# A transformer kernel on one core: planner prices, two tables of plan parameters, and the place of one load

## The chip, the cores and the metric

The kernel runs on one core of one Trainium2 chip. The metric is the time of one execution on the device in microseconds (us). The kernel before took 3521.76, 3529.83 and 3524.83 us in three runs, a median of 3524.83 us.

## What is computed

Two transformer blocks over a sequence of 1024 tokens and a width of 1024, everything in float32. The first block has eight heads of latent attention, eight heads of dilated attention and sixteen experts. The second block has two layers, and each of them three kinds of attention over one projection. Cut to what matters here:

```python
def second_block(x, ctx, ...):
    for l in range(2):
        qa, ka, va, ga, qb, kb, vb, gb, qn, kn, vn, gn = split_proj(h @ w_in[l])
        # A: differential attention, 4 heads, 1024 + 256 context keys
        a = softmax(q0 k0) - lam * softmax(q1 k1);  oa = a @ va
        ya = rms_norm(oa, diff_subln[l]) * (1 - lam_init) * silu(ga)
        # B: grouped-query attention, 6 heads over 2 K/V heads
        yb = gqa_attend(qb, kb_all, vb_all) * silu(gb)
        # C: neighbourhood attention, 6 heads, windows of 8 x 16 in a grid, and the context
        yn = neighbourhood_attend(qn, kn, vn, kn_c, vn_c, nat_rpb[l], rows) * silu(gn)
        x = x + gt * (concat([ya, yb, yn]) @ w_out[l])
        # layer 0 also computes the three attentions for 256 context queries
```

## The kernel before

The program is a row of stages: the first block's projection, its attention, output projection, router and experts, and then for each layer of the second block a projection (`proj2`), the attention (`attn2`) and the output projection. The projections are long rows of matrix multiplications of split weights. They write their results into the arrays partA, partB, partC and the stacks of queries and keys in device memory, with stores (L1671, L1788) that the SyncE queue (SP) issues; the attention loads its tiles from there (L1936 for values and gates, L1943 for queries and keys, the latter on GpSimd's queue, POOL).

Inside an attention stage nobody writes the order of the instructions by hand. Each small group of instructions is an operation that is handed to a planner with `pl.op(prio, eng, fn, deps, bufs, dma)`: a priority, the engines that can do it with a price in microseconds for each, the function that issues it, the operations that it needs, its buffers, and the time of a transfer. `Plan.run` (L156) then goes through a simulated time: whenever an engine is free by the prices, it takes the ready operation with the lowest priority number whose buffers are free, and issues it. On every engine but SP the order so found is fixed. The prices and the priorities therefore set the order of the work, though not the time that it takes on the chip. Ahead of `run`, `Plan.early` (L144) issues a list of loads, which stand in front of everything in the plan.

The priorities come from the streams. In `attn2_open` (L1851) a layer has a stream "x", which holds three pairs of heads of the neighbourhood attention (`nat_tile`, L2301, 48 tiles) and then three of the grouped-query attention (`gqa_group`, L2232), and a stream "d" with the four heads of the differential attention (`stream_d`, `d_tile`). `TUNE` (L34) holds a row of parameters for each plan, "first" for the first block's attention and 0 and 1 for the layers: `lead` is how much earlier a load is wanted than its use, `aS`, `aD`, `aN` pull scores ahead, `pvx` and `pvd` push the multiplication by V back, `d0` and `df` set the start and speed of stream "d", `s`, `t` and `o` are how many banks of PSUM a kind of tile may hold.

Some names that the rest speaks of. xq, xk, xv and xP are the queries, keys, values and scores of stream "x", dq, dk, dv and dP those of "d"; s, w, t and o are tiles in PSUM: scores (s for "x", w for "d"), transposes (t) and outputs (o). L2323 makes a neighbourhood tile's scores, L2330 and L1933 on VectorE (DVE) their maxima, L2346 on ScalarE (ACT) the exponential; L317 is the transpose on TensorE (PE) and L2280 the multiplication by V. L2240, L2244 and L2245 make scores for the grouped-query heads (L2244 and L2245 as a pair into a t tile), L1030 is DVE's maximum over them, L1063 and L1067 what ACT and POOL or DVE do with the probabilities, L1998 their multiplication by V. L2092, L2096 and L2101 are the differential attention's scores, maxima and exponentials; L2032 and L2033 combine its two maps on POOL (L2030 is the same on DVE). At the end of each of its heads `d_finish` (L2145) computes a norm: a square on POOL (L2152), then on DVE a sum (L2156) and in `rstd_v` (L1837) thirteen operations (L1841 to L1848) on 128 x 10 numbers, as one operation of the plan with a price of 1.7 us, and then products on POOL (L2160).

The first value tile of stream "x", xv, is loaded by an operation in `pair` (inside `stream_x`, L2184), with a priority `lead` ahead of its use; the list that goes to `early` holds the keys, queries and tables (tb) of the first pair. Its buffers come out of pools by tag: xk, xq and tb from a pool (`ax1`) that is opened during the projection, all others from one that opens with the attention.

## Time and profile before

| | us |
|---|---|
| median of three runs | 3524.83 |
| lowest, highest run | 3521.76, 3529.83 |
| the profiled execution, its own time | 3530.24 |
| its span in the trace | 3528.2 |
| PE busy | 3339.7 (95%) |
| DVE busy | 2286.2 (65%) |
| ACT busy | 1711.5 (49%) |
| POOL busy | 1271.4 (36%) |
| mean granted clock of PE | 0.974 |

The profile shows one execution. Its span runs from the first to the last instruction, its own time also has what lies around them. Stages are told apart by their lines: the first block's attention lies between 255 and 865 us, layer 0's attention between 1905 and 2456, layer 1's between 2960 and 3424. In a list of waits, each row names the engine and the line that waited, the engine and result that ended the wait, the total, the number of times and the longest. In a timeline the columns are start, duration, engine, line, operation and tiles, and in brackets the idle time of the engine just ahead, with what ended it.

### The profile page before, as it was taken

The numbers are of one execution on the slowest core, as the hardware profiler recorded it, in microseconds if no ns is written. First come the engines' busy times: TensorE is split into PE (matmuls) and PEld (weight loads), VectorE is DVE, ScalarE is ACT, GpSimd is POOL, SyncE is SP. The second block draws the span as 40 slices with busy tenths as digits, with TensorE's granted clock in tenths as the row PEclk, the third lists the DMA queues.
The fourth block names the chain that finished last, engine by engine and source line by source line (L and its number), as shares of the span: only waits on it lengthen the run. The fifth ranks groups of instructions, "written<-read, shape, count | busy, mean of one in ns | idle before, by whom it ended". The sixth has DMA issues, their size and how long they took to land.

```text
span 3528.2 us, 50927 instructions
## 1 busy us (share of the span) xinstructions
PE 3339.7 (95%) x17832; PEld 2568.6 (73%) x17832; DVE 2286.2 (65%) x4884; ACT 1711.5 (49%) x3154; POOL 1271.4 (36%) x1103
## 2 busy tenths in 40 slices
PE   6998999988799999989999989999999999999999
PEld 5987666656588887779888665556899888765567
DVE  5524546544799998876770777876446821888762
ACT  4423545432388877753222666654333222776640
POOL 3211334332001010023451466756333521557761
PEclk9999999999899999999999999999999999999999
DMA  7338778575799999854353643114334354551133
GB/s 208 84 116 229 184 201 225 169 220 197 285 383 398 393 380 376 311 160 126 113 154 107 150 117 81 39 41 128 120 128 131 112 153 105 128 122 44 40 111 114
DMA packets 402451, 606.97 MB, mean 172 GB/s; under 512 B 77554, under 2 KB 283506, under 8 KB 398098
## 3 DMA queue, kind: packets, MB, share of 16 engines
q1 hardware_dynamic: 342772, 492.56, 41.9%
q0 software_dynamic: 26240, 94.13, 11.3%
q10 hardware_dynamic: 33184, 17.04, 1.7%
q8 instruction: 141, 2.31, 0.3%
q14 instruction: 114, 0.93, 0.1%
HBM read 479.10 MB, written 124.55 MB: 171 GB/s over the span
## 4 chain that ended last, share of the span: by engine, by line
PE 61%; DVE 7%; issue 2%; DMA 2%; POOL 2%; ACT 1%; SPq 0%; ACTq 0%; DVEq 0%; POOLq 0%
PE s L350 7%; PE t L317 6%; PE s L351 6%; PE s L349 6%; PE a L350 6%; PE a L351 6%; PE a L349 6%; PE o L1998 5%; PE o L2280 2%; PE w L2092 2%; PE s L2240 2%; PE s L2323 2%; PE t L2244 1%; PE t L2245 1%; PE t L2006 1%
## 5 line engine op out<-in xcount | busy, mean ns | idle before, releaser
L349 PE MATMUL a<-wh,h2H 128*128 128x384 f32 (+2 forms) x1280 | 460.5, 360 | 7.3 <-ACT wh L334 7.3
L1544 DVE TENSOR_TENSOR wl<-wr,wh 128x1024 fp32r<-128x1024 f32 x384 | 450.3, 1221 | 25.9 <-ACT wh L1543 19.3
L350 PE MATMUL a<-wl,h2H 128*128 128x384 f32 (+2 forms) x1280 | 453.7, 355 | 3.0 <-POOL wl L336 1.6
L351 PE MATMUL a<-wh,h2L 128*128 128x384 f32 (+2 forms) x1280 | 453.3, 354 | 1.7 <-POOL h2L L603 1.7
L1543 ACT ACTIVATE wh<-wr 128x1024 fp32r<-128x1024 f32 x384 | 394.7, 1058 | 75.2 <-PE s L351 73.7
L349 PEld LDWEIGHTS a<-wh,h2H 128*128 128x128 f32 x1280 | 243.1, 190 | 28.5 <-ACT wh L334 8.2
L350 PEld LDWEIGHTS a<-wl,h2H 128*128 128x128 f32 x1280 | 243.1, 190 | 24.9 <-POOL wl L336 2.5
L351 PEld LDWEIGHTS a<-wh,h2L 128*128 128x128 f32 x1280 | 242.6, 190 | 23.7 <-POOL h2L L603 2.1
L1067 POOL TENSOR_TENSOR xP<-xP,xPT 128x512 f32<-128x512 f32 x134 | 189.3, 1415 | 52.6 <-ACT xPT L1063 31.5
L350 PE MATMUL s<-wl,xH 128*128 128x512 f32 x512 | 202.0, 395 | 5.6 <-DVE wl L1544 5.2
L349 PE MATMUL s<-wh,xH 128*128 128x512 f32 x512 | 202.1, 395 | 0.0
L351 PE MATMUL s<-wh,xL 128*128 128x512 f32 x512 | 199.9, 390 | 0.0
L2096 DVE CUSTOM_DVE_ANT_0 dP<-w,zero 128x1280 f32<-128x1280 f32 x128 | 190.0, 1484 | 12.7 <-PE w L2092 9.9
L2101 ACT ACTIVATE dP<-dP,d 128x1280 f32<-128x1280 f32 x128 | 174.3, 1362 | 24.4 <-DVE d L2096 23.5
L1030 DVE TENSOR_REDUCE x<-s 128x1 f32<-128x512 f32 (+1 forms) x240 | 158.1, 684 | 31.9 <-PE s L2240 31.2
L1063 ACT ACTIVATE xPT<-t 128x512 f32<-128x512 f32 x240 | 132.1, 599 | 91.1 <-PE t L2245 78.5
L349 PE MATMUL s<-wh,yoH 128*128 128x512 f32 x416 | 167.6, 404 | 2.6 <-ACT wh L334 1.7
L336 POOL TENSOR_TENSOR wl<-wr,wh 128x1024 fp32r<-128x1024 f32 (+3 forms) x43 | 94.3, 2194 | 201.4 <-ACT wh L334 191.3
L350 PE MATMUL s<-wl,yoH 128*128 128x512 f32 x416 | 166.0, 399 | 0.8 <-DVE wl L336 0.8
L351 PE MATMUL s<-wh,yoL 128*128 128x512 f32 x416 | 165.1, 397 | 0.0
L1526 POOL DMA_INDIRECT xg<-h2d,idx x16 | 16.8, 1050 | 399.2 <-PE t L317 325.1
L336 DVE TENSOR_TENSOR wl<-wr,wh 128x1024 fp32r<-128x1024 f32 (+3 forms) x55 | 70.8, 1289 | 120.3 <-ACT wh L334 120.3
(463 smaller groups left out, 8363.8 us busy)
## 6 DMA issues: line engine op xcount, KB each, us to landing
wr<-in_w_gate_dram SPq DMA_DIRECT2D x128, 512.0 KB
wr<-in_w_up_dram SPq DMA_DIRECT2D x128, 512.0 KB
wr<-in_w_down_dram SPq DMA_DIRECT2D x128, 512.0 KB
aw<-in_w_ada_dram SPq DMA_DIRECT2D x32, 1024.0 KB
wr<-in_w_in_dram SPq DMA_DIRECT2D x50, 512.0 KB
aw<-in_w_ada_dram SPq DMA_DIRECT2D x32, 512.0 KB
wr<-in_w_in_dram SPq DMA_DIRECT2D x40, 384.0 KB
xk<-stackCk POOLq DMA_DIRECT2D x24, 640.0 KB, 10.6
```

What stands on the lines that cost most here:

```text
L317: self.nc.tensor.transpose(out, in_, self.ident[:n, :n])
L336: e.tensor_tensor(l, raw, h.bitcast(F32), ALU.subtract)
L349: nc.tensor.matmul(out, sH, h, start=first, stop=False)
L350: nc.tensor.matmul(out, sH, l, start=False, stop=False)
L351: nc.tensor.matmul(out, sL, h, start=False, stop=last)
L1030: nc.vector.tensor_reduce(dst, Sb.t[:, :n * w].rearrange("p (k c) -> p k c", k=n) if n > 1 else Sb.t[:, :w], AX.X, ALU.max)
L1067: eng.tensor_tensor(A.t[:, :512], PT.t[:, 0, :] if kb == 1 else A.t[:, :512], PT.t[:, kb, :], ALU.add)
L1543: nc.scalar.activation(h, raw, AF.Copy)
L1544: nc.vector.tensor_tensor(l, raw, h.bitcast(F32), ALU.subtract)
L1998: nc.tensor.matmul(O.t[a * 64:(a + 1) * 64, :], v(kb), PT[0](kb), start=(kb < 2), stop=(kb >= nb - 2))
L2096: nc.vector.tensor_tensor_reduce(Ps[i].t, W.t[:, :1280], self.zero.to_broadcast([P, 1280]), -1.0, 3e38, ALU.add, ALU.min, m["m"])
L2101: nc.scalar.activation(Ps[i].t, Ps[i].t, AF.Exp, bias=m["m"], scale=-1.0, accum_out=box[j][:, i:i + 1])
```

## The change

Three things change. The parameters of layers 0 and 1 in `TUNE` get new values. Prices of seven kinds of PE operation get new values; four of these (`st_group`, the transposes, the multiplications by V and the transposes back) are used in the first block's attention too, whose parameters stay as they are. And the first V tile moves into the pool that is open early, and its load into the list that is issued ahead of the plan. Cut to its core:

```diff
-    0: dict(lead=22.2, aS=54.6, aD=15.2, aN=47.2, st=0.4, pvx=21.6, pvd=16.7, d0=37.1, df=0.53, s=2, t=6, o=6),
-    1: dict(lead=13.3, aS=103.7, aD=14.6, aN=39.8, st=0.2, pvx=28.2, pvd=79.2, d0=14.4, df=0.5, s=2, t=4, o=2),
+    0: dict(lead=46.6315, aS=54.6, aD=17.6065, aN=54.9623, st=0.1169, pvx=20.343, pvd=0, d0=38.1898, df=0.53, s=2, t=9, o=4),
+    1: dict(lead=43.3625, aS=124.3762, aD=110.0272, aN=62.8556, st=0.1161, pvx=30.4682, pvd=59.8728, d0=10.0665, df=0.5317, s=2, t=4, o=7),
...
-            return pl.buf(tag, stream, lambda i: (pools.get(tag) or pools.get(tag[0]) or pools[rest]).tile(
+            return pl.buf(tag, stream, lambda i: (pools.get(f"{tag}{i}") or pools.get(tag) or pools.get(tag[0]) or pools[rest]).tile(
...
-                o = pl.op(p - self.q["aS"], {"pe": 0.02 + n * w * 0.0005}, mm, lds, [Sb] + QK)
+                o = pl.op(p - self.q["aS"], {"pe": 0.06 + n * w * 0.0005}, mm, lds, [Sb] + QK)
...
-        self.pools = {"xk": x1, "xq": x1, "tb": x1}
+        self.pools = {"xk": x1, "xq": x1, "tb": x1, "xv0": x1}
...
-            o = pl.op(p, {"pe": m * 0.107}, tr, [dep], [T, Pt, PT])
+            o = pl.op(p, {"pe": m * 0.115}, tr, [dep], [T, Pt, PT])
...
-            o = pl.op(p, {"pe": 0.89}, mm, list(deps) + [o], [O] + V)
+            o = pl.op(p, {"pe": 0.96}, mm, list(deps) + [o], [O] + V)
...
-        o = pl.op(p, {"pe": 1.7 if den else 0.8}, back, [o] + (den[0] if den else []), [oT, T] + (den[2] if den else []))
+        o = pl.op(p, {"pe": 1.0 if den else 0.84}, back, [o] + (den[0] if den else []), [oT, T] + (den[2] if den else []))
...
-            o = pl.op(p - self.q["aD"], {"pe": 0.71}, mm, lds, [W, Q, K])
+            o = pl.op(p - self.q["aD"], {"pe": 0.74}, mm, lds, [W, Q, K])
...
+                loads.append(vs[kind, p][1])
...
-        return loads[:5]
+        return loads[:6]
...
-        o = self.st_group("x", 2.95, 10, CH, s1, st, 0.43, [Q, K], [lq, lk, lm], Qm, lambda: Qm.t[64:68, i, :],
+        o = self.st_group("x", 2.95, 10, CH, s1, st, 0.5, [Q, K], [lq, lk, lm], Qm, lambda: Qm.t[64:68, i, :],
...
-        o = pl.op(p - self.q["aN"], {"pe": 0.88}, scores, [lq, K[0][1], K[1][1]], Sb + [Q, K[0][0], K[1][0]])
+        o = pl.op(p - self.q["aN"], {"pe": 1.9}, scores, [lq, K[0][1], K[1][1]], Sb + [Q, K[0][0], K[1][0]])
```

Lines from 2184 on stand one line further down in the changed kernel. The instructions are the same in both; what changes is where they stand. Two places are shown.

The first place is SP's queue where layer 0's attention begins (partA to partC are stores of the projection, vd its output tiles, dv, xv and xg loads of values and gates). Before:

```order
L1878 DMA subln_18174<-in_diff_subln_dram 128x64
L1671 DMA partC<-vd_18155 128x384
L1936 DMA dv_18191<-partA 128x10x64
L1936 DMA xv_18180<-partC 128x10x128
L1936 DMA xg_18185<-partC 128x4x128
L1936 DMA xgx_18187<-partC 128x2x128
```

And with the change, where the load of xv now stands, further up in the queue:

```order
L1788 DMA stackBk<-sL_17465 128x128
L1671 DMA partA<-vd_17503 128x256
L1936 DMA xv_17510<-partC 128x10x128
L2200 DMA tb_17518<-in_c_rpb_dram 128x1600
L2200 DMA tb_17520<-in_c_rpb_dram 128x1600
L1671 DMA partA<-vd_17556 128x256
```

The load of xv has moved from behind the projection's last store to a place ahead of both tables and of 21 stores.

The second place is PE where the fourth head of the differential attention ends in layer 0 (its DVE block, L2156 to L1848, is issued meanwhile). Before, the last result that DVE takes ahead of the block is the score tile s_22663, and PE's rows from there to these hold it, four pairs L2244 and L2245 and two short scores; these are the last twelve rows up to the first score tile (s_22745) that needs DVE after the block:

```order
L2245 MATMUL t_22685<-tb_22079,xk_20512 128x512
L2240 MATMUL s_22689<-xk_20805,xq_22481 128x512
L2244 MATMUL t_22691<-xq_22047,xk_20512 128x512
L2245 MATMUL t_22691<-tb_22079,xk_20512 128x512
L2244 MATMUL t_22713<-xq_22047,xk_20512 128x512
L2245 MATMUL t_22713<-tb_22079,xk_20512 128x512
L2244 MATMUL t_22718<-xq_22047,xk_20512 128x512
L2245 MATMUL t_22718<-tb_22079,xk_20512 128x512
L2398 MATMUL o_22722<-xPT_22465,xv_20018 64x256 x4
L317 MATMUL t_22733<-ident,sl_22605 4x128
L1998 MATMUL o_22735<-xPT_22574,xv_20018 64x512 x2
L2240 MATMUL s_22745<-xk_20805,xq_22481 128x512
```

With the change, from the last result that DVE takes ahead of the block (s_22723) to the first score tile that needs DVE after it (s_22789):

```order
L2241 MATMUL s_22723<-xk_20818,xq_22442 128x512
L317 MATMUL t_22727<-ident,oT_22593 128x128 x2
L317 MATMUL t_22735<-ident,sl_22601 4x128
L2241 MATMUL s_22737<-xk_20818,xq_22442 128x512
L1998 MATMUL o_22743<-xPT_22606,xv_20046 64x512 x2
L2241 MATMUL s_22747<-xk_20818,xq_22442 128x256 x2
L1998 MATMUL o_22743<-xPT_22606,xv_20046 64x512 x2
L2245 MATMUL t_22771<-xq_21990,xk_20818 128x512
L2246 MATMUL t_22771<-tb_22027,xk_20818 128x512
L1998 MATMUL o_22743<-xPT_22606,xv_20046 64x512 x4
L2241 MATMUL s_22789<-xk_20818,xq_22442 128x512
```

Seven pairs of score rows stood in this stretch before, and one stands there now, with eight steps of a multiplication by V.

## Rows read from the trace of the kernel before

**Rows 1.** Page, part 1: busy time, share of the span, instructions of each engine.

```profile
PE 3339.7 (95%) x17832; PEld 2568.6 (73%) x17832; DVE 2286.2 (65%) x4884; ACT 1711.5 (49%) x3154; POOL 1271.4 (36%) x1103
```

**Rows 2.** Windows: length, busy PE, PEld, DVE, ACT, POOL, granted clock, DMA share, GB/s.

```profile
255.00:865.00 610.00, 555.70 (x3185) 390.74 (x3184) 309.79 (x793) 258.54 (x658) 199.17 (x185) 0.95 0.71 204
1905.00:2456.00 551.00, 514.02 (x2855) 337.39 (x2853) 411.20 (x951) 322.17 (x647) 329.94 (x303) 0.96 0.35 88
...
2960.00:3424.00 464.00, 452.43 (x2568) 295.29 (x2567) 362.87 (x855) 300.47 (x563) 298.79 (x265) 0.99 0.38 96
```

**Rows 3.** Waits of PE, layer 0's attention, the longest and one other.

```profile
PE t L317 <- ACT xP L2346: 6.5, 5, 3.6
PE o L2280 <- DMA xv<-partC: 5.5, 1, 5.5
...
PE t L317 <- DVE xy L1073: 3.2, 1, 3.2
```

**Rows 4.** Waits of PE, layer 1's attention, the longest.

```profile
PE t L317 <- ACT xP L2346: 3.5, 3, 2.6
```

**Rows 5.** The chain of waits at layer 0's start.

```profile
1935.27 14.73 DMA xv<-partC
```

**Rows 6.** Timeline of PE at layer 0's start.

```profile
1950.14 1.12 PE L2280 MATMUL o<-xPT,xv 128*64 128x256 f32 x4 [5.49 <-DMA xv<-partC]
...
1957.51 0.98 PE L317 MATMUL t<-ident,xP 128*128 128x128 f32 x7
```

**Rows 7.** Timeline of SP's queue ahead of layer 0's attention.

```profile
1905.30 25.28 SPq L1671 DMA_DIRECT2D partC<-vd  x7
```

**Rows 8.** Timeline of all engines at layer 0's start, POOL and ACT.

```profile
1948.04 0.17 POOL L2351 MEMSET xP<- 128x64 f32 x1
...
1954.97 1.03 ACT L2346 ACTIVATE xP<-xP,x 128x896 f32<-128x896 f32 x1
```

**Rows 9.** Windows of 5 us at layer 0's start, the one behind the wait.

```profile
1950.00:1955.00 5.00, 4.86 (x24) 2.76 (x24) 1.24 (x6) 0.53 (x2) 0.15 (x1) 0.65 1.10 236
```

**Rows 10.** Timeline of DVE, the four ends of a head in layer 0.

```profile
2079.87 0.81 DVE L2156 TENSOR_REDUCE ass<-dg 128x10 f32<-128x640 f32 x1
...
2081.73 2.77 DVE L1843 TENSOR_SCALAR vr<-vt 128x10 int32<-128x10 int32 x1
...
2186.05 1.30 DVE L1842 TENSOR_SCALAR vt<-vv 128x10 int32<-128x10 int32 x1
...
2272.19 2.59 DVE L1841 TENSOR_SCALAR vv<-ass 128x10 f32<-128x10 f32 x1
2274.82 0.17 DVE L1842 TENSOR_SCALAR vt<-vv 128x10 int32<-128x10 int32 x1
...
2371.77 1.13 DVE L1843 TENSOR_SCALAR vr<-vt 128x10 int32<-128x10 int32 x1
```

**Rows 11.** Timeline of POOL beside the first of them.

```profile
2081.54 2.92 POOL L2033 TENSOR_TENSOR dP<-dP,dP 128x1280 f32<-128x1280 f32 x1
```

**Rows 12.** Timeline of PE behind the four ends of a head.

```profile
2088.15 1.76 PE L317 MATMUL t<-ident,xP 128*128 128x128 f32 x7 [3.61 <-ACT xP L2346]
...
2189.79 0.80 PE L2244 MATMUL t<-xq,xk 128*128 128x512 f32 x1 [3.37 <-DVE dPT L1929]
...
2277.70 0.75 PE L2116 MATMUL s<-dk,dx 96*128 96x256 f32 x2 [2.31 <-DVE x L1030]
...
2375.40 0.73 PE L2240 MATMUL s<-xk,xq 128*128 128x512 f32 x2 [1.29 <-DVE x L1030]
```

**Rows 13.** The chain of waits: durations of PE groups in layer 0.

```profile
2207.27 0.24 PE t L2245
2207.51 1.01 PE o L1998 x4
...
2210.92 2.31 PE s L2378 x8
```

**Rows 14.** Waits of PE, the first block's attention, the longest for another engine.

```profile
PE t L317 <- DVE sL L671: 7.2, 1, 7.2
```

## The prediction, before the changed kernel was run

> **What bounds the kernel now.** The page's first lines come first: TensorE (PE) is busy 95% of the span, no other engine over 65% [rows 1]. So an edit is worth what it does to PE's idle time, and to the clock that PE is granted. Next the stages. The change touches three: the first block's attention, and the attention of layer 0 and of layer 1 of the second block. PE is idle for 610.0 - 555.7 = 54.3 us in the first, 551.0 - 514.0 = 37.0 us in layer 0 and 464.0 - 452.4 = 11.6 us in layer 1; the granted clock is 0.95, 0.96 and 0.99 [rows 2]. A clock of 0.96 over 551 us is 22 us lost in layer 0, so there a microsecond of idle time comes with 22 / 37.0 = 0.6 us of lost clock, and in layer 1 with 4.6 / 11.6 = 0.4 us. I use these two factors below.
>
> Third, PE's waits. Layer 0 has one wait for a transfer, 5.5 us for the first V tile (xv), and many short ones for VectorE (DVE) and ScalarE results [rows 3]. Layer 1 has the same kinds, shorter, and no wait for xv [rows 4].
>
> **Term 1: the first V tile is loaded ahead.** Before, SP issues this load at 1935.27, behind the last store of the projection and the load of dv; it takes 14.73 us and lands as PE starts on it at 1950.14, after 5.49 us with nothing to do [rows 5, 6]. In the new order the load stands on SP ahead of both tables (tb), five stores of partA, eight of partB and eight of partC (first pair of order rows above), which is at least 25 us, the time that SP spends on the last seven partC stores [rows 7]; 14.73 us fit in that. So this wait goes. Behind it on SP stand the tables and the stores; V's columns were stored in an earlier pass, so on SP it has to wait for nothing later than the store eight rows ahead of it. What is late next? POOL clears a strip (L2351) of a later score tile at 1948.04, since its queue holds that behind loads of dq and dk; ScalarE then needs 1.03 us for the tile, and PE transposes it, at 1957.51 in the old trace, 7.4 us after V [rows 6, 8]. With V there and at full clock the nine PE groups in between take some 5 us, so PE comes there at 1944.7 + 5 = 1949.7, and the tile is ready at 1948.2 + 1.0 = 1949.2: hidden by half a microsecond, and up to 2 us of wait come back if POOL or DVE is later. The stall also cost clock: in the 5 us after it the granted clock is 0.65 with PE busy for 4.86 [rows 9], which is 4.86 x 0.35 = 1.7 us lost. The term is -5.5 - 1.7 = **-7.2 us**; bounds -8.5 (the clock dip gone wholly, and work behind it earlier) and -2 (the strip and the dk loads hold PE instead). I take -7.2, since the new order also places other work there and the strip just fits.
>
> In layer 1 nobody waits for V [rows 4]: 0.
>
> **Term 2: where a head of the differential attention ends.** Four times per layer DVE runs a block of 14 operations (L2156, L1841 to L1848) on ten numbers a row, during which nothing it owes PE gets done. A small operation of it takes 0.17 us, but in each of the four blocks one was stretched, to 2.77, 1.30, 2.59 and 1.13 us [rows 10]; the first of them lies beside a POOL combine (L2033) of 2.92 us and ends with it [rows 11]. Behind the four blocks of layer 0 PE stood 3.61, 3.37, 2.31 and 1.29 us, 10.6 in all [rows 12]. The planner still prices the block at 1.7 us, in both versions, so where it falls is not arranged. I counted from the two orders how much PE work lies between the last PE result that DVE takes ahead of the block and the first PE instruction that needs something DVE makes after it, with the durations of PE's rows, such as 0.24 us for a score row of 512 columns and 1.01 us for four o steps [rows 13]. For layer 0's fourth block (second pair of order rows above): before, the fourteen rows of t (L2244, L2245) make 3.4 us and the others 1.6, 5.0 in all; now three small transposes, eight o steps and the score rows make 0.3 + 2.0 + 1.0 = 3.3 us. All four blocks: 5.1, 3.1, 4.5 and 5.0 us of cover before, 2.9, 2.8, 4.7 and 3.3 us now, so 17.7 us become 13.7. What DVE has to do in that time falls only from 22.0 to 21.2 us by the mean durations of its lines. The shortfall grows from 4.4 to 7.5 us, so 3.2 us more idle, by the factor 1.6 **+5.1 us**. Layer 1 by the same count goes from 4.4 to 5.5: +1.1 by 1.4, **+1.5 us**. Bounds: 0 (other work was put in front) and +16 (rival C).
>
> By the rows the stretch is a matter of what POOL happens to do at that moment: it runs from 1.13 to 2.77 us [rows 10], 7.8 us in the four blocks of layer 0, and I hold it at that. The Trainium skill (SBUF — State Buffer, Who interferes with whom) says that VectorE and GpSimd share a port pair as an exclusive lock, so that a VectorE operation in a two-port mode or with two inputs in SBUF waits for the whole GpSimd instruction, while a reduction never does. The trace agrees: L2156, a reduction, takes its usual 0.81 us, and the tensor_scalar operations behind it are those stretched. By that rule every block that meets a combine pays up to its whole 2.92 us, 11.7 us for the four, which speaks against a plan with less cover: 3.9 us more than the sum has. Rival C works this out from rows.
>
> **Term 3: the rest of layer 0's idle time.** 37.0 - 5.5 - 10.6 = 20.9 us in waits of up to 3.2 us, as that for xy [rows 3]. They are the planner's misjudgements of what is ready when, and the prices that now change were among the worst: the eight context-score multiplications that it took for 0.88 us take 2.31, now 1.9; a pair of grouped-query score rows takes 0.24 + 0.24, priced 0.43, now 0.5 [rows 13]. For a gain: layer 1, the same kind of work, has 11.6 us idle in 464. Against: the neighbourhood tiles whose PE cover between scores and transposes is under 3.5 us go from 7 to 12 of 48 by the two orders; PE's waits for such tiles are 6.5 us in 5 [rows 3], so five more could cost 5 x 1.3 x 1.6 = +10 us. DVE's and POOL's prices, 75% and 60% busy here [rows 2], were not corrected. Bounds: -20.9 x 1.6 = -33 and +10. I take a quarter of the idle time off, -5.2 x 1.6 = **-8.4 us**, nearer to zero than to the end, since prices of PE alone are only part of what the planner gets wrong.
>
> **Term 4: the first attention.** Its parameters stay, but its order moves with the prices of shared helpers. PE's longest wait for another engine there is 7.2 us, at the stage's start, outside the plan [rows 14]; a plan that is not searched again may win or lose about one such wait: 0, bounds -8 and +8. All other stages: unchanged instructions, 0.
>
> **Sum.** -7.2 + 5.1 + 1.5 - 8.4 + 0 = -9.0 us. The profiled execution took 3530.24 us (span 3528.2), so 3521.2; it is 5.4 us above the median of the three runs, 3524.83, so the median should come to **3515.8 us**. What a measurement can tell from no change is some 0.2%, 7 us.
>
> **Rivals.**
> - **B, the wait for V is replaced and the rest cancels.** PE gets V and soon stands before the tile whose strip POOL clears at 1948.04: term 1 is -2, and terms 2 to 4 sum to 0. For it: POOL's queue there is unchanged by the load [rows 8]. Against: only one tile hangs on that strip. About 3522.8 (-6 to +4).
> - **C, slower: the head ends.** The shortfall of 4.4 us by median durations became 10.6 us of waiting, a factor of 2.4, through POOL combines beside the block. The same factor makes 7.5 x 2.4 = 18.1 us in layer 0 (+7.5) and +1.1 x 2.4 = +2.6 in layer 1; with lost clock 10.1 x 1.6 = +16, less the 7 of V: +9, **3533.8 us**. It decides from the point at which PE waits over 18 us behind the four blocks of layer 0 with nothing won elsewhere. Against it: which combine meets which block is drawn anew.
> - **D, a large gain.** Layer 0 falls to layer 1's loss: (11.6 + 4.6) x 551 / 464 = 19 us in place of 37 + 22 = 59, so -40, or half of it. For it: the two layers do the same work but for the context queries, and layer 1's plan shows that such an order exists. Against: DVE is more loaded in layer 0. About 3495 (-15 to -40).
>
> **How the numbers follow.** Forecast 0.46, with a range of its own of 3511 to 3521; B 0.22, C 0.14, D 0.18. Of the forecast's cases some six in ten lie beyond 7 us: 0.30, with D's 0.18 faster 0.48. Of C some seven in ten are over +7 us: slower 0.10. Same: the remaining 0.42. The range takes in the forecast, B, most of C and D's upper third: 3502 to 3532, leaving out some 0.12 below and 0.07 above.
>
> **What would show it.** Right: in the profile of the changed kernel no wait of PE for xv, the granted clock of the stage's first 30 us at 1.00, idle time in layer 0 near 30 us, with waits behind L1841 to L1848 of 11 us or more, layer 1's idle near 12. Wrong: a new wait of over 2 us for xP at the first V group (B); over 18 us behind the four blocks (C); layer 0 idle under 22 us (D); or the first attention moved by over 8 us, which the sum holds at zero.

## The result, and the profile after

The changed kernel took 3544.98 us, the median of 6 runs (3537.14 to 3546.93), against 3525.97 us of the kernel before in 6 runs beside it. The ratio is 1.0054, with a 95% interval from 1.0043 to 1.0065: it is **slower by 19 us**, where 9 us less was forecast. The profiled execution took 3544.16 us (span 3542.2).

The three stages by windows of the changed kernel, in the columns of [rows 2]:

```profile
255.00:881.00 626.00, 559.08 (x3183) 393.36 (x3182) 314.50 (x801) 254.83 (x651) 200.16 (x187) 0.93 0.71 199
1921.00:2463.00 542.00, 511.23 (x2877) 337.30 (x2875) 404.15 (x939) 324.16 (x654) 340.16 (x310) 0.97 0.37 92
...
2967.00:3438.00 471.00, 455.14 (x2569) 294.19 (x2568) 374.37 (x863) 296.84 (x553) 304.33 (x266) 0.99 0.37 93
```

Each stage ends where its work ends, so the lengths can be compared with [rows 2]: the first attention is 16 us longer (626 for 610), with 66.9 us of PE idle for 54.3 and a granted clock of 0.93 for 0.95. Layer 0 is 9 us shorter (542 for 551), idle 30.8 for 37.0, clock 0.97 for 0.96. Layer 1 is 7 us longer, idle 15.9 for 11.6, and DVE is busy 374 us there for 363. Since a window's borders are set by hand, from here on a stage is measured between the last split product of the projection ahead of it and the first one behind it: before 427.4, 527.5 and 452.3 us, after 442.9, 516.2 and 458.8. Before:

```profile
331.70:759.10 427.40, 395.68 (x2355) 260.78 (x2353) 233.04 (x621) 199.18 (x529) 160.59 (x153) 0.95 0.71 197
1933.50:2461.00 527.50, 490.20 (x2723) 313.47 (x2721) 411.85 (x954) 319.63 (x642) 330.94 (x304) 0.95 0.36 92
2975.30:3427.60 452.30, 440.65 (x2496) 283.11 (x2494) 364.65 (x859) 299.68 (x562) 300.42 (x266) 0.99 0.39 97
```

After, the two layers (the first attention's row stands with run 1):

```profile
1951.60:2467.80 516.20, 485.43 (x2723) 311.50 (x2721) 405.21 (x942) 321.82 (x650) 340.89 (x311) 0.97 0.38 96
2982.40:3441.20 458.80, 442.94 (x2496) 281.99 (x2494) 375.91 (x865) 296.63 (x553) 305.83 (x266) 0.98 0.37 95
```

The stretches in between are alike (1174.4 and 1176.3 us from the first attention to layer 0).

PE's waits in layer 0 of the changed kernel, those that answer to [rows 3]:

```profile
PE w L2092 <- DVE d L2096: 5.2, 4, 4.4
PE s L2324 <- DVE xPT L1929: 4.3, 1, 4.3
PE t L317 <- ACT xP L2347: 3.8, 5, 1.1
```

The wait for xv of 5.5 us is gone, and no transfer stands among the longest. Behind the four ends of a head, to be set against [rows 12]:

```profile
2092.59 0.64 PE L2324 MATMUL s<-xk,xq 128*128 128x320 f32 x1 [4.26 <-DVE xPT L1929]
...
2187.30 0.50 PE L2245 MATMUL t<-xq,xk 128*128 128x512 f32 x1 [2.51 <-DVE x L1030]
...
2289.43 0.79 PE L2092 MATMUL w<-dk,dq 96*128 96x512 f32 x1 [4.38 <-DVE d L2096]
...
2385.56 0.73 PE L2241 MATMUL s<-xk,xq 128*128 128x512 f32 x2 [0.17 <-DVE x L1030]
```

In the first attention PE's waits for another engine now look so:

```profile
PE t L317 <- ACT oT L1927: 6.5, 1, 6.5
PE t L994 <- ACT oT L1927: 6.2, 1, 6.2
...
PE s L990 <- DVE m L1030: 5.7, 2, 4.8
```

None of these three stood in the trace before. The loss is in the stage that the sum held at zero, so its waits come first.

**The first one, on ScalarE's queue.** Timeline of ACT around the first wait (ACTq: transfers issued on ACT's queue):

```profile
458.68 1.36 ACTq L501 DMA_DIRECT2D mod<-am  x4
469.93 0.39 ACTq L1939 DMA_DIRECT2D yd<-my  x1
470.37 0.38 ACT L1927 ACTIVATE oT<-o 128x256 f32<-128x256 f32 x1 [13.20 <-DMA aw<-in_w_ada_dram]
```

And the load in question in SP's queue, and PE:

```profile
457.95 0.33 SPq L464 DMA_DIRECT2D aw<-in_w_ada_dram  x1
...
470.81 0.69 PE L317 MATMUL t<-ident,oT 128*128 128x128 f32 x2 [6.48 <-ACT oT L1927]
```

A store of one finished tile (yd) stands on ACT ahead of the copy oT. The program deals eight completion counters in turn to the transfers that SP and ACT issue. By its own list of waits this store waits, beside DVE's result, for the earlier transfer that had the counter before it: the load of a megabyte of modulation weights (aw) that SP issued at 457.95. ACT computes nothing for 13.2 us, in which four stores (mod) take 1.36 us and the rest passes until that load has landed; PE's transpose, which needs only the copy behind the store, waits 6.48 us. The second wait has another form: at 711.67 eight small stores of modulation rows (mod) hold ACT's queue for 5.99 us, 0.75 us each, and the copy behind them comes at 717.76.

```profile
711.67 5.99 ACTq L518 DMA_DIRECT2D mod<-am  x8
717.76 0.38 ACT L1927 ACTIVATE oT<-o 128x256 f32<-128x256 f32 x1 [8.55 <-DMA mod<-am]
718.20 0.80 PE L994 MATMUL t<-mq,mk 96*128 96x512 f32 x1 [6.24 <-ACT oT L1927]
```

The planner prices a store of a finished tile at 0.1 us of ACT, and these eight together at 0.5. The trace before has a stall of the first kind too: ACT stood 9.6 us until a load of aw had landed, and PE 3.3 us behind the copy that came late by it. From the lists of waits of ACT and of PE in its first attention:

```profile
ACT mq L1055 <- DMA aw<-in_w_ada_dram: 9.6, 1, 9.6
```

```profile
PE t L996 <- ACT mq L1055: 3.3, 1, 3.3
```

**The second kind, DVE beside POOL.** DVE's and POOL's timeline ahead of the third wait, and PE:

```profile
549.89 6.06 DVE L1262 TENSOR_TENSOR eC<-eC,jB 128x512 f32<-128x512 f32 x1
...
551.11 3.04 POOL L1262 TENSOR_TENSOR eC<-eC,jB 128x512 f32<-128x512 f32 x3
...
558.76 0.68 DVE L1262 TENSOR_TENSOR eA<-eA,jA 128x512 f32<-128x512 f32 x1
...
561.37 0.80 PE L990 MATMUL s<-mk,mq 96*128 96x512 f32 x1 [4.84 <-DVE m L1030]
```

One multiplication on DVE took 6.06 us next to POOL's multiplications, where the same operation alone takes 0.68; DVE worked without a gap from there to the maximum that PE waits for, so that was late by as much.

**And the clock.** Windows around the end of the first wait (470.81) and right behind it, the granted clock third from the end:

```profile
467.00:477.00 10.00, 6.19 (x26) 5.46 (x26) 4.12 (x13) 3.33 (x11) 0.00 (x0) 0.53 0.63 193
471.00:475.00 4.00, 4.00 (x15) 3.62 (x15) 3.26 (x11) 1.71 (x8) 0.00 (x0) 0.50 0.83 299
```

For 4 us behind the wait PE is busy throughout, at the lower of its two clocks (0.50).

### The profile page after: what moved, and what is told of

It reads as the page before. It is cut to its first block, busy times and chain, and to the rows that moved or that the text cites. A ratio compares the mean times of both kernels' runs of the same rounds, so it can differ in the third digit from the quotient of the medians.

```text
span 3542.2 us, 50954 instructions
## 1 busy us (share of the span) xinstructions
PE 3342.1 (94%) x17832; PEld 2570.0 (73%) x17832; DVE 2294.0 (65%) x4885; ACT 1706.3 (48%) x3144; POOL 1288.9 (36%) x1112
## 3 DMA queue, kind: packets, MB, share of 16 engines
q0 software_dynamic: 26240, 94.13, 11.4%
## 4 chain that ended last, share of the span: by engine, by line
PE 60%; DVE 9%; issue 2%; ACT 2%; POOL 1%; DMA 1%; SPq 0%; ACTq 0%; DVEq 0%; POOLq 0%
PE s L350 7%; PE s L351 7%; PE s L349 7%; PE t L317 7%; PE a L351 5%; PE a L350 5%; PE a L349 5%; PE o L1998 5%; PE o L2281 2%; PE w L2092 2%; PE s L2324 2%; PE s L2241 2%; PE t L2245 1%; PE t L2246 1%; PE t L2006 1%
## 5 line engine op out<-in xcount | busy, mean ns | idle before, releaser
L1544 DVE TENSOR_TENSOR wl<-wr,wh 128x1024 fp32r<-128x1024 f32 x384 | 450.1, 1219 | 26.5 <-ACT wh L1543 18.9
L350 PEld LDWEIGHTS a<-wl,h2H 128*128 128x128 f32 x1280 | 243.0, 190 | 24.9 <-POOL wl L336 2.4
L351 PEld LDWEIGHTS a<-wh,h2L 128*128 128x128 f32 x1280 | 242.5, 190 | 23.5 <-POOL h2L L603 2.1
L2033 POOL TENSOR_TENSOR dP<-dP,dP 128x1280 f32<-128x1280 f32 x54 | 160.0, 2963 | 4.5
```

Of the source, the lines that this page charges most:

```text
L350: nc.tensor.matmul(out, sH, l, start=False, stop=False)
L351: nc.tensor.matmul(out, sL, h, start=False, stop=last)
L1544: nc.vector.tensor_tensor(l, raw, h.bitcast(F32), ALU.subtract)
L2033: nc.gpsimd.tensor_tensor(P0.t[:, a], P0.t[:, a], P1.t[:, b], ALU.add)
```

## The experiments

In the kernels made for these, each plan has a row of its own prices, and a flag tells whether its first V tile is loaded ahead, so that each stage can be given the old or the new plan by itself. Their code differs from the changed kernel in this, and beyond it only as shown:

```diff
-                o = pl.op(p - self.q["aS"], {"pe": 0.06 + n * w * 0.0005}, mm, lds, [Sb] + QK)
+                o = pl.op(p - self.q["aS"], {"pe": self.q["P"]["st"] + n * w * 0.0005}, mm, lds, [Sb] + QK)
...
-                loads.append(vs[kind, p][1])
+                self.q["va"] and loads.append(vs[kind, p][1])
```

In runs 8 to 13 lines from L501 on stand one line further up. All medians are set against runs of the kernel before on the same chip.

| run | median us | before | ratio, 95% interval | first att. | layer 0 | layer 1 |
|---|---|---|---|---|---|---|
| changed kernel | 3544.98 | 3525.97 | 1.0054 (1.0043 to 1.0065) | 442.9 | 516.2 | 458.8 |
| 1, old first attention | 3523.53 | 3524.91 | 0.9997 (0.9988 to 1.0006) | 421.0 | 515.9 | 458.3 |
| 2, early V alone, both layers | 3546.41 | 3524.91 | 1.0063 (1.0049 to 1.0076) | 423.6 | 522.8 | 468.4 |
| 3, new layer 0 alone | 3517.29 | 3524.91 | 0.9976 (0.9967 to 0.9985) | 422.0 | 514.2 | 450.1 |
| 4, one price put right | 3535.76 | 3524.91 | 1.0023 (1.0013 to 1.0033) | 433.8 | 517.6 | 454.8 |
| 5, early V, layer 0 alone | 3518.94 | 3525.59 | 0.9984 (0.9971 to 0.9997) | 422.8 | 522.0 | 451.5 |
| 6, old plans nudged | 3526.39 | 3525.59 | 1.0001 (0.9987 to 1.0016) | 424.5 | 527.0 | 450.0 |
| 7, new plans nudged | 3522.91 | 3525.59 | 0.9990 (0.9975 to 1.0005) | 420.1 | 518.7 | 459.9 |
| 8, fewer stores | 3521.48 | 3525.59 | 0.9985 (0.9973 to 0.9997) | 434.8 | 519.8 | 455.8 |
| 9, as 3, fewer stores | 3509.51 | 3524.80 | 0.9950 (0.9937 to 0.9964) | 420.2 | 516.3 | 451.9 |
| 10, before, fewer stores | 3519.22 | 3524.80 | 0.9980 (0.9969 to 0.9991) | 420.3 | 527.9 | 451.2 |
| 11, as 1, fewer stores | 3512.99 | 3526.79 | 0.9965 (0.9951 to 0.9978) | 420.5 | 515.0 | 459.2 |
| 12, as 9, head end priced | 3497.13 | 3526.79 | 0.9910 (0.9897 to 0.9923) | 421.3 | 507.6 | 451.0 |
| 13, as 12, in both layers | 3499.67 | 3526.79 | 0.9923 (0.9910 to 0.9936) | 417.0 | 508.0 | 454.9 |

The last three columns are from one profile each. The old order of the first attention came to between 417.0 and 427.4 us in ten profiles, so a difference of 4 us in one stage says little.

**Run 1: the first attention planned with the old prices.**

```diff
     "first": dict(lead=23.3, ..., s=4, t=7, o=2,
+        P=dict(st=0.02, pv=0.89, bk=1.7)),
```

> The changed kernel, but the first block's attention is planned with the old prices, so that its order is that of before; both layers as changed. Theory R (the loss is the first attention's redrawn order, which no search has followed): that stage goes back from 626 to 610 us, the layers keep their times, so 3545 - 15.5 = about 3529 (3526 to 3533). Rival S (the loss is a side effect of the new place of V or of the layers' plans, such as other transfers in the way): no return, 3538 or more.

Measured 3523.5: the stage went from 442.9 to 421.0 us, and the layers kept theirs. Its window, and below it that of the changed kernel, with borders set by the same rule:

```profile
328.70:749.70 421.00, 391.59 (x2355) 260.33 (x2354) 233.43 (x621) 198.94 (x529) 160.41 (x153) 0.96 0.71 200
```

```profile
332.40:775.30 442.90, 399.75 (x2355) 263.52 (x2353) 237.93 (x629) 195.59 (x522) 162.25 (x155) 0.93 0.70 190
```

The changed order costs 43.1 - 29.4 = 13.7 us of idle time, and PE is busy 8.2 us longer with the same 2355 instructions, at a clock of 0.93 for 0.96. Together 21.9, near the 21.5 us between the medians. That they agree so well is partly luck: run 1's profiled execution is the fastest of its eleven (3516.5 us). Over the five profiles of the old order with 32 stores the difference is 11.4 to 13.7 us of idle time and 4.1 to 8.2 us of busy time. 3523.5 lies just below the text's range, which was worked out from the one profile of before. Theory R holds as to the place; S falls.

**Runs 2 and 5: early V alone.** Old prices and parameters, with the V tile loaded ahead in both layers, and then in layer 0 alone:

```diff
+    0: ... va=1      1: ... va=1     (run 2)
+    0: ... va=1      1: ... va=0     (run 5)
```

> The kernel before with only the first V tile loaded ahead in both layers; prices and parameters are the old ones. As predicted for this term: the wait of 5.5 us and the clock behind it go, 3526 - 7.2 = about 3519 (3517 to 3522). Rival B: the wait is replaced by one for the next score tile, 3524 (3522 to 3527).

> The kernel before with the first V tile loaded ahead in layer 0 alone, layer 1 planned as before. Theory R (an order that no search has followed costs 10 to 20 us per stage by chance; early V also takes one load out of the plan and so redraws the order): layer 0 some 5 us shorter as in the run with V in both layers, layer 1 back at 450 to 452 us, in all 3525 - 5 = 3520 (3515 to 3524). Rival V (loading V ahead itself slows the kernel, for instance by holding SP or memory): 3535 or more.

In layer 0 the order on PE stays the same instruction by instruction, and the stage goes from 527.5 to 522.8 and 522.0 us. Run 5's window of layer 0:

```profile
1926.20:2448.20 522.00, 490.81 (x2722) 315.45 (x2721) 409.65 (x954) 320.32 (x643) 330.90 (x304) 0.96 0.37 94
```

Idle is 522.0 - 490.8 = 31.2 us, 6.1 less than before (527.5 - 490.2 = 37.3), and PE's busy time is the same. So the wait went and nothing took its place; Rival B falls. But in layer 1, where nobody waits for V, the same edit made the stage 16 us longer in the profile (run 2):

```profile
2969.70:3438.10 468.40, 444.81 (x2495) 278.93 (x2494) 387.09 (x868) 295.32 (x551) 298.07 (x262) 0.99 0.37 93
```

Idle is 23.6 us there against 11.7 before. With the load out of the plan, the planner had the V tile at its time zero and made another order: at most 58% of PE's instructions there stand in the old sequence (the longest common sequence of the two programs, by the names of the tiles). An input that comes earlier made a list-scheduled plan longer. Neither text foresaw this: run 2's total of 3546 is far outside both.

**Run 3: the new plan in layer 0 alone** (first attention and layer 1 with old prices and parameters, `va=0` in layer 1).

> The kernel before with the new prices, new parameters and early V in layer 0 alone; the first attention and layer 1 as before. Theory R: layer 0 keeps the 11 us that it gains in the changed kernel's trace, 3526 - 11 = about 3515 (3512 to 3518), faster than both kernels; with the first run it leaves +6 for layer 1's new plan (3529 against 3515 + 8 at most). Rival S: no gain beyond that of V alone.

3517.3, inside R's range: the new layer 0 is worth 7.6 us in the medians and some 11 in the profiles with this plan (8 to 13), 5 of it early V. Against run 1 (the same but for layer 1) the new layer 1 costs 6.2 us.

**Run 4: one price of the first attention put back.** In both traces PE needs a median of 1.72 to 1.77 us for the transposes back with their denominators (L1077 and L2006 of the first attention). The change prices them at 1.0:

```diff
-        P=dict(st=0.06, pv=0.96, bk=1.0)
+        P=dict(st=0.06, pv=0.96, bk=1.7)
```

> The changed kernel with one price in the first attention put back: the transposes back with the denominator at 1.7 us, which is what they take in both traces (median 1.72 to 1.77 us), where the change prices them at 1.0. Theory P (this one wrong price spoils the plan): the first attention returns to about 610 us, 3530 (3526 to 3534). Theory R (any redrawn order with the old parameters loses about as much): 3537 to 3550, no nearer to before than by chance.

3535.8 lies between the two texts: 9 of the 21 us came back, with the stage at 433.8.

```profile
331.90:765.70 433.80, 399.63 (x2354) 261.69 (x2352) 234.75 (x624) 198.14 (x524) 162.89 (x154) 0.93 0.70 194
```

Idle fell by 9 us to 34.2, and the lost clock stayed: PE is busy 399.6 us, as in the changed kernel. The order costs 11 us still. Since the price draws the order anew, the run does not show whether the right price or the new draw brought the 9 us back.

**Runs 6 and 7: nudges.** One parameter moved by about 1% in each plan.

```diff
-  "first": df=0.886   0: df=0.53   1: df=0.5                       (old plans, run 6)
+  "first": df=0.880   0: df=0.535  1: df=0.505
-  "first": d0=22.1    0: df=0.53   1: df=0.5317                    (old first, new layers, run 7)
+  "first": d0=22.6    0: df=0.535  1: df=0.5367
```

> The kernel before, old prices, no early V, with one parameter per plan moved by about 1%: df 0.886 to 0.880 in the first attention, 0.53 to 0.535 in layer 0, 0.5 to 0.505 in layer 1. Nothing is cheaper or dearer by this; only the order is drawn anew. Theory R: the stages are longer than before (421 to 427, 527 and 450 to 452 us between the projections' last and first split products) by 5 to 20 us each, the sum by 15 to 40: 3540 to 3565. Theory P (prices decide, orders near by are alike): all within 4 us, 3521 to 3529.

> Another draw: the first attention with old prices and d0 22.1 to 22.6; layer 0 and layer 1 as in the changed kernel (new prices, new parameters, early V) with df 0.53 to 0.535 and 0.5317 to 0.5367. Theory R: layer 0 loses most of what its new table gained, 516 to 525 us or more, layer 1 stays at 455 to 470, the first attention at 430 to 445. Theory P: layer 0 stays at 514 to 518, the first attention at 421 to 428.

The orders did change (in the three stages 77 to 97% of PE's instructions keep the old sequence, by the same count), and the time did not: 3526.4, and 3522.9 beside the 3523.5 of run 1. Theory R in its wide form, that any order which no search has followed costs 10 to 20 us, falls. The share of the order that is kept says nothing either: of the first attention's order run 6 keeps 77% and loses nothing, the changed kernel keeps 78% and loses 21 us, run 4 keeps 83% and loses 11. What is left, and these runs do not show it by themselves, is that a few instructions come to stand behind a wait that the planner does not know.

**Runs 8 to 11: the stores on ScalarE's queue.** The changed kernel, with the modulation rows stored by one transfer for each run of rows, 10 in place of 32; inside the stage PE's order stays as it is, instruction by instruction:

```diff
-            for j in range(4):
-                q.dma_start(self.mod1[g * 4 + j:g * 4 + j + 1, :], r[32 * j:32 * j + 1, :])
+            q.dma_start(self.mod1[g * 4:g * 4 + 4, :], r[0:97:32, :])
...
-            for j, (l, c) in enumerate(pieces):
+            for j, l, c, n in runs:
                 for w in range(2):
-                    q.dma_start(self.mod2[(l * 2 + w) * 6 + c:(l * 2 + w) * 6 + c + 1, :],
-                                           r[32 * j + 16 * w:32 * j + 16 * w + 1, :])
+                    q.dma_start(self.mod2[(l * 2 + w) * 6 + c:(l * 2 + w) * 6 + c + n, :],
+                                           r[32 * j + 16 * w:32 * (j + n - 1) + 16 * w + 1:32, :])
```

> The changed kernel, with the stores of the modulation vectors from the first attention (L501, L518, issued on ScalarE's queue) made with one transfer per run of rows in place of one per row, 10 in place of 32; everything else in the plan is priced and ordered as in the changed kernel. Theory M (the redrawn order puts ScalarE's copies that PE needs behind stores on ScalarE's in-order queue, each waiting for an earlier transfer): the waits for oT of 6.5 and 6.2 us shrink, the first attention from 443 to 430 to 437 us, in all 3533 to 3539. Rival (the stores only stand where ScalarE would wait anyway): 3542 to 3547.

3521.5: the loss of the change was gone, and more than expected. PE's waits in the first attention of this run:

```profile
PE s L989 <- DVE m L1029: 5.7, 2, 4.8
PE t L993 <- ACT oT L1926: 3.6, 1, 3.6
```

Of the two waits behind stores one is gone and the other went from 6.2 to 3.6 us; the wait behind the stretched multiplication stayed, as it should. How the first one went is seen on ACT:

```profile
460.10 0.36 ACTq L1938 DMA_DIRECT2D yd<-my  x1
460.50 0.38 ACT L1926 ACTIVATE oT<-o 128x256 f32<-128x256 f32 x1 [6.55 <-DMA aw<-in_w_ada_dram]
```

With fewer transfers ahead of it the same store of yd has another of the eight counters, and by the program's list of waits it now waits for the load of aw before the one it had waited for: ACT computes nothing for 6.55 us in place of 13.20. So the edit did two things at once: it took 22 transfers away, and it dealt the counters anew to all transfers behind them. The two were not tried apart. The stage's window:

```profile
328.40:763.20 434.80, 403.69 (x2363) 263.81 (x2362) 239.26 (x630) 197.05 (x524) 162.17 (x155) 0.93 0.71 197
```

Idle went from 43.1 to 31.1 us, near that of the old order, while the clock stayed at 0.93 and PE is busy 403.7 us. But the stage explains only 8 of the 23.5 us. Another 10 came off the stretch behind it, up to layer 0, from 1176.3 to 1165.8 us. So the merged stores were tried in other orders too.

> The kernel with the new plan in layer 0 alone (first attention and layer 1 planned as before), with the modulation stores merged from 32 to 10 transfers. The run with fewer stores shortened two stretches of the changed kernel, the first attention by 8 us and what follows it up to layer 0 by 10. If the second part belongs to the stores and not to that order, this run has it too: 3517 - 10 = about 3507 (3503 to 3511), the fastest yet. If both parts came from the changed order alone: 3515 to 3519.

> The kernel before with nothing but the merged modulation stores. Theory M in its narrow form (the stores cost the first attention only where the new order puts ScalarE's copies behind them): the first attention stays at 421 to 427 us, and only the stretch behind it shrinks by 8 to 10 us: about 3516. In its wide form (the stores hold ScalarE in any order): the first attention falls below 418 us too, 3508 or less.

> The changed kernel with the first attention in its old order (as in the first run) and with the 10 merged stores: the fourth corner of a square of two orders of the first attention by 32 or 10 stores, the layers being the same in all four. Known: old order, 32 stores 3523.5; new order, 32 stores 3545; new order, 10 stores 3521.5. Theory M (32 stores cost far more in the new order, by standing ahead of copies that TensorE waits for): the stores are worth only some 6 us in the old order, as in the kernel before, so 3517.5 (3514 to 3520), and the new order is left with 4 us of loss without them. Rival (the stores are worth about as much in either order): 3500 to 3506.

They are worth 5.6 us to the kernel before (run 10), 7.8 to run 3 (run 9) and 10.5 to run 1 (run 11), with the first attention at 420.3, 420.2 and 420.5 us as without them. The gain lies behind that stage: with 32 stores the stretch took 1174.0 to 1176.6 us in nine profiles, with 10 stores 1165.8 to 1170.3 in five of six, and 1174.9 in the sixth. There the order is not the same: with 10 stores the output projection begins with sixteen transposes of finished tiles (yo), with 32 it begins with eight and has the other eight, and a short wait for them, between its products. PE there in the kernel before, and in run 10:

```profile
757.34 1.94 PE L317 MATMUL t<-ident,yo 128*128 128x128 f32 x8 [6.70 <-DMA yo<-yd]
...
763.58 1.10 PE L317 MATMUL t<-ident,yo 128*128 128x128 f32 x8 [0.45 <-DMA yo<-yd]
```

```profile
750.63 3.36 PE L317 MATMUL t<-ident,yo 128*128 128x128 f32 x16 [6.26 <-DMA yo<-yd]
```

PE's wait for cx (L1314) further on is 5.9 to 6.7 us in all nine profiles with 32 stores and 3.5 in all six with 10. So a part of what the merged stores gain in any order of the first attention goes with this other order behind it (and eight transposes more count to the stage); how much of it is not shown. The square of run 1, the changed kernel, run 8 and run 11 then reads: 32 stores cost 23.5 us in the new order and 10.5 in the old one, the new order costs 21.5 us with 32 stores and 8.5 with 10. Set against the kernel before on each chip, with intervals of 3 to 5 us either way, the four are +19.0, -4.1, -1.4 and -13.8 us, which makes 23 and 12, 20 and 10. The text for run 11 had 3517.5, and 3513.0 lies just below its range. So some 11 to 13 us of the loss go with the 32 stores in that order, and some 8 to 10 are left. In what is left PE is busy 403.7 us in run 8 and 392.2 in run 11, at a clock of 0.93 and 0.96; why the clock is lower there is open, and the stretched multiplication was not taken out by itself.

**Runs 12 and 13: the end of a head priced.** Layer 0 (and in run 13 layer 1, with early V) planned with DVE's block at 4.4 us, the transposes back at 1.7, and parameters searched anew for the shortest plan on these prices:

```diff
-        o = pl.op(p, {"dve": 1.7}, sums, [o], [G_])
+        o = pl.op(p, {"dve": self.q["P"].get("fin", 1.7)}, sums, [o], [G_])
...
+    0: dict(lead=49.0918, aS=61.7492, aD=18.5415, aN=50.3697, st=0.2241, pvx=21.3918, pvd=3.3136, d0=43.5788, df=0.5301, s=2, t=3, o=5, ... fin=4.4),
+    1: dict(lead=53.1289, aS=106.1488, aD=113.434, aN=57.5556, st=0, pvx=31.8869, pvd=60.5614, d0=11.2562, df=0.5174, s=2, t=5, o=6, ... fin=4.4),   (run 13)
```

> The fastest kernel so far (new plan in layer 0 alone, 10 stores; 3509.5) with layer 0 planned once more: DVE's block at the end of a head of the differential attention priced at 4.4 us (it took 4.4 to 6.5 us in the traces) in place of 1.7, the transposes back at 1.7, and layer 0's parameters searched on these prices. Theory H (the stalls behind the four blocks, 10.6 us before and 11.2 us in the changed kernel, come from that price): they fall below 6 us, layer 0 from 516 to about 508, in all 3501 (3498 to 3505). Rival (which POOL operation stands beside the block decides, and the planner does not see it): stalls of 9 us and more, layer 0 at 513 to 520, 3506 to 3513.

> The same in both layers, layer 1 with early V and parameters searched on the same prices. In the changed kernel layer 1 lost about 6 us against its old plan (457 against 451). If that loss comes from the wrong prices on which its table was searched (transposes back at 1.0, the block at 1.7), it goes: layer 1 at 445 to 452, the total at most that of the run before it. If the old plan of layer 1 was a lucky order that no prices lead to, layer 1 stays at 455 to 460 and the total is 5 to 9 us above the run before it.

Run 12 took **3497.1 us**, 29.7 us less than the kernel before, and is the fastest of all; the text's range began at 3498. Layer 0 is 507.6 us long for 516.3 in run 9. Where PE stood behind the four blocks in run 9, and where in run 12:

```profile
2065.38 0.90 PE L2323 MATMUL s<-xk,xq 128*128 128x320 f32 x2 [4.25 <-DVE xPT L1928]
...
2160.14 0.50 PE L2244 MATMUL t<-xq,xk 128*128 128x512 f32 x1 [2.50 <-DVE x L1029]
...
2262.32 0.79 PE L2091 MATMUL w<-dk,dq 96*128 96x512 f32 x1 [4.37 <-DVE d L2095]
```

```profile
2158.11 0.51 PE L2115 MATMUL s<-dk,dx 96*128 96x256 f32 x2 [1.95 <-DVE x L1029]
```

With 0.17 us behind the fourth block, 11.3 us have become 2.5, of which 1.95 stand in this one row. The second block was stretched worse than any before it, twice over:

```profile
2151.57 2.61 DVE L1840 TENSOR_SCALAR vv<-ass 128x10 f32<-128x10 f32 x1
2154.22 1.20 DVE L1841 TENSOR_SCALAR vt<-vv 128x10 int32<-128x10 int32 x1
```

But the first and the third block met no POOL operation this time and took 3.28 us each, where in run 9 they took 6.02 and 6.51 us, and 8.1 of the 8.8 us that went had stood behind these two. The first block's first operation in run 9, and in run 12:

```profile
2059.82 2.92 DVE L1840 TENSOR_SCALAR vv<-ass 128x10 f32<-128x10 f32 x1
```

```profile
2061.55 0.17 DVE L1840 TENSOR_SCALAR vv<-ass 128x10 f32<-128x10 f32 x1
```

So run 12 by itself does not decide between Theory H and its rival, though its time is Theory H's. Run 13's trace speaks for H: in layer 1 three of the four blocks were stretched three times over, to 6.18, 5.70 and 6.34 us for 3.10 of the first, and PE stood 1.0 us behind one of them and not at all behind the other two. In the changed kernel blocks of 4.07 and 4.21 us in layer 1 had cost 2.28 and 1.25 us. The fourth block in run 13:

```profile
3330.65 1.23 DVE L1841 TENSOR_SCALAR vt<-vv 128x8 int32<-128x8 int32 x1
...
3332.00 1.28 DVE L1843 TENSOR_SCALAR vv<-vv 128x8 f32<-128x8 f32 x1
...
3333.38 1.25 DVE L1846 TENSOR_TENSOR vt<-vt,vv 128x8 f32<-128x8 f32 x1
```

There the collisions still happen, and PE has other work in hand. The whole of layer 0's idle time fell less than the waits behind the blocks, from 29.6 to 24.9 us: 3.3 us of wait for DVE's xP (L1066) are new. The transposes' price and the search changed with the block's price, and the three were not tried apart. Run 13 gives layer 1 454.9 us and a total 2.5 us above run 12, between its two texts: of the 6 us that the new layer 1 lost, some came back, and the old plan of layer 1 stays the best that ran.

## Why the prediction was wrong

- **Term 4, the first attention: the step that failed.** It was held at 0, with 8 us either way, on the ground that "a plan that is not searched again may win or lose about one such wait". It measured +21.5 us by run 1; with run 3's -7.6 for layer 0 and 6.2 for layer 1 that makes +20, against the +19 measured. The prediction itself named a move of this stage by over 8 us as a sign of being wrong. Three things went past the sentence on one wait. The prices in this plan did not all move towards the trace: the transposes back went from 1.7 to 1.0 where they take 1.72, and the order drawn with that put right lost 9 us less. ACT's queue was not looked at as one that also issues stores which wait for other transfers, and some 11 to 13 us of the loss go with those. The trace before had such a stall too, with 9.6 us on ACT and 3.3 us on PE. And the bounds of 8 us count no lost clock: 4 to 8 of the 22 us are PE busy longer at a lower clock. It does not simply go with the idle time, for in runs 4 and 8 idle fell by 9 and 12 us and the clock stayed at 0.93; what lowers it is open.
- **Term 1, early V: right.** -7.2 forecast; runs 2 and 5 show 5 us in the stage, run 5 6.7 us in the medians. The idle time went as forecast (5.5 forecast, 6.1 measured); the 1.7 us of clock did not show in PE's busy time. That V in layer 1 costs "0" was wrong by way of the plan: with the old parameters it cost 16 us (run 2).
- **Term 2, the ends of the heads: the mechanism right, the size off.** PE's idle time behind layer 0's four blocks went from 10.6 to 11.3 us, not up by 3.2; layer 1's from 2.5 to 4.5. The cover was counted wrong: one row of the order for a multiplication by V or a transpose back (L1998, L2280, L2398, L2006) is two records in the trace, so the 1.01 us of [rows 13] are two steps and not four. The eight steps in the fourth block's new cover then make some 4.0 us and not 2.0, the cover some 5.3 us and not 3.3 (an estimate from [rows 13]), and PE waited 0.17 us there. The covers before grow too, by six such steps in the fourth block. The lock between DVE and POOL that the Trainium skill states (SBUF — State Buffer, Who interferes with whom) is seen again, for the tensor_scalar operations of the block (2.61 us in run 12) and for a product of two tiles (6.06 us); the trace agrees also in that the reduction ahead of the block took its 0.81 us each time. The 6.06 us go further than the rule as it is put: they are longer than any one POOL operation beside them and end behind the fifth of five that POOL ran in a row from 550.11 to 555.40. A block can also meet more than one operation: two of the four blocks before had a second stretched one (0.77 and 0.70 us) that the count left out.
- **Term 3, the rest of layer 0: the sum right by luck.** -8.4 was forecast; terms 1 to 3 of layer 0 sum to -10.5 and the stage became 11.3 us shorter in the profile (8 to 13 in the other runs with this plan). But term 2 was too high by some 4 us, and of the part beyond V and the head ends the idle time gave only some 1.8 us; 4.8 us are PE busy for less time, at a clock of 0.97 for 0.95.
- **Layer 1:** +1.5 forecast for the head ends; it lost 6 us (runs 1 and 3), with 4.2 us more idle, 2.0 of it behind the head ends, and DVE 11 us longer busy. Where the rest comes from was not tried.
- **The rivals.** C has the sign, but not by its mechanism: 11.3 us behind the four blocks is far from the 18 at which it was to decide. B and D are excluded by run 5 and by layer 0's 30.8 us of idle time.

## What to carry to other kernels

Where an order is planned on prices, compare every changed price with the trace that is at hand, and give the operations that a plan holds for nearly free (a store on an in-order engine, a chain of tiny operations next to another engine's large one) what they take at their worst. A plan made with one of them priced had 8.8 us less of such waits on PE and took 12 us less in all (run 12 against run 9), though the price was not the only thing that changed. A plan that shares helpers with the one being tuned is changed too, and has to be measured as a stage of its own; so has each edit that only makes an input come earlier. Idle time of TensorE is not the whole of a loss: in the first attention 13.7 us of it came with 8.2 us of longer busy time at a lower clock, and the second part stayed when most of the first had gone. And an edit that takes transfers away also deals out the completion counters anew and can redraw the order of the stage behind it, so the time that it gains is not by itself the price of the transfers.

## What was not expected of the hardware

- A store of a finished tile on ScalarE's queue waited until a one-megabyte load that it has nothing to do with had landed, and ScalarE computed nothing for 13.2 us; with another of the eight counters the same store cost 6.55 us.
- A DVE multiplication of two SBUF tiles took 6.06 us next to POOL's multiplications, for 0.68 alone, and a block of tiny DVE operations was hit twice in a row (2.61 and 1.20 us).
- The stalls of one order are repeated almost to the hundredth from run to run: behind the ends of the heads 4.26, 2.51 and 4.38 us in the changed kernel, 4.25, 2.50 and 4.37 in run 9, which has the same plan in that layer.
- The trace has 17832 records of PE where the program has 15944 matrix multiplications and transposes. The 1888 more are the products of plain float32 operands (the multiplications by V and the transposes back among them), each of which shows as two; products of operands marked float32r, and transposes, show as one.
